# Up-projection of a gated-linear-attention encoder: the two features of a group half a group apart

## The chip, the cores and the metric

The kernel runs on one core of one Trainium2 chip. The metric is the device time of one execution in microseconds (us); the median of three runs is taken. All matmuls are float32 split by hand into a high and a low part (hi, lo), three matmuls for one product.

## What is computed

One encoder layer on a sequence of 2048 tokens of 1024 numbers: a gated linear attention, then a feed-forward net with a causal convolution, each with a norm and a residual, and a last norm. The change lies in the feed-forward net:

```python
def causal_dwconv(u, w, b):
    K = w.shape[0]
    L = u.shape[1]
    up = jnp.pad(u, ((0, 0), (K - 1, 0), (0, 0)))
    out = up[:, K - 1:K - 1 + L] * w[K - 1] + b
    for k in range(K - 1):
        out = out + up[:, k:k + L] * w[k]
    return out

def conv_ffn(h, w_up, conv_w, conv_b, w_down):
    u = causal_dwconv(h @ w_up, conv_w, conv_b)
    g, val = jnp.split(u, 2, axis=-1)
    return (jax.nn.silu(g) * val) @ w_down
...
    x = x + conv_ffn(h, ffn_w_up[i], ffn_conv_w[i], ffn_conv_b[i], ffn_w_down[i]).astype(x.dtype)
return rmsnorm(x, final_norm_w)
```

w_up has 1024 x 5632 entries, w_down 2816 x 1024, the convolution three taps.

## The kernel before

**Stages.** The attention's projections run as four passes (R, A, B, Y) over eight pairs of 128-token tiles; then comes the up-projection (`phase_u`), from 894 us on, and from about 1790 us the down-projection with the last norm. Every large matrix product is done by Winograd's form of Strassen's scheme: a product of 2 x 2 blocks by seven block products p1 to p7 in place of eight, with sums and differences of blocks as operands. A block product is 12 matmuls of 128 x 128 by 128 x 512 (`mm3p`, lines 177 to 179: four steps of the contraction, three matmuls each).

**The up-projection.** The sequence is done in two halves (s = 0, 1) of 1024 tokens. In a half, 22 features are worked, a feature being 128 gate columns with the 128 value columns that belong to them; two features make a group (11 groups). The tokens' operands, one of two hi/lo tiles for each of the seven products, stay on chip for a half (`hop`, filled by `load_op` from the scratch `hd`, 2 MB a product). The weights' operands are made in place: `load` brings four raw 128 x 512 blocks a feature (`ur`), and `prep` forms the sum or difference on POOL, casts the high part on ACT (line 186) and takes the low part on DVE (line 187, `split`). `prep` runs five products ahead.

**Order before.** In a group the order is p1, p5, p6, p7, p4, p2, p3, each for the even feature and then for the odd one. Two PSUM banks collect a feature: bank a takes p1, p6, p7 and p4, one on top of the other, bank c takes p5 and then p3; p2 has a bank of its own. Between the steps the running sums are read out: ACT copies bank a after p1 (c1), p6 (c2) and p7 (u3) and, after p4, into the value's tile; DVE adds make the even or odd 128-token blocks of the gate's u and of the value's u. A matmul that adds to a bank must wait until the read of the step before is done.

**Convolution.** When a feature's value (after p4) or gate (after p3) is complete, `conv` follows at once: one ACT activation (last tap and bias, line 1235), two DVE taps (line 1237), and for the gate a silu on ACT (line 1239). After the gate's, `gated` multiplies (line 1244), stores two blocks of the result to the scratch `ad` and, for an odd feature, forms four sums on POOL and stores them for the down-projection.

**The second half's operands.** While the first half runs, `prep_h2` makes the operands of the second half from the tokens' rows: for each of four pairs of tiles nine steps (a load, seven operands, a last store), with a difference and a low part on DVE and a cast on ACT. `spread` deals them out by a clock that the program keeps for itself while it is written out (`adv`, `later_do`): the first step 14.0 us behind the opening of the buffers, then one each 11.0 us (`U0`, `U1`), wherever that falls in the group. Their results lie in the ring of six tiles "as", which the POOL sums and u3 use too, and are stored to `hd` by DMAs that ACT issues.

**Queues.** Each engine carries out its instructions in the order in which the program issues them, DMA issues among them: an issue that must wait holds up what the program put behind it on that engine. SP issues the raw loads, the operand loads and the stores of `ad`; ACT issued the stores of `hd`.

**The ends.** The operands of the first half are loaded during the last pass Y, in that pass's order of products (p1, p5, p6, p7, p4, p2, p3). Near the end of the second half `d_early` starts the down-projection: loads of w_down into operand tiles that are free, and four prepared steps.

## Time and profile before

| | us |
| --- | --- |
| median of three runs | 2225.44 |
| lowest and highest run | 2217.04, 2226.30 |
| profiled execution, its own time | 2224.22 |
| its span, first to last instruction | 2222.5 |
| mean granted TensorE clock | 0.986 |

A row of the chain or of the timeline gives start, duration (both us), engine, line, operation, the tile written and those read, shape and count; the bracket is the engine's idle time before it and what ended it. A row of groups gives count, busy time, mean duration in ns and the idle time before. A row of the waits gives who waited for whom, the total in us, how often, and the longest. A row by stretch gives start and end, length, then for each engine the busy time and the number of instructions, at the end the granted TensorE clock, the DMA engines' busy share and GB/s. PE is TensorE (PEld its weight loads), DVE VectorE, ACT ScalarE, POOL GpSimd, SP the sync engine; a q behind the name means its sequencer, which issues DMAs.

### The profile page before, as it was taken

How to read it: one execution, taken by the hardware profiler on the slowest of the kernel's cores; microseconds unless marked ns; L12 is line 12 of the kernel's file. 1: busy time of each engine (PE TensorE's matmuls, PEld its weight loads, DVE VectorE, ACT ScalarE, POOL GpSimd, SP SyncE). 2: the span in 40 equal slices, each digit the busy share in tenths (PEclk: the TensorE clock that was granted, in tenths of full speed). 3: DMA queues.
4: the chain of work that ended last, by engine and by line, in shares of the span. 5: the costliest groups of instructions: out<-in, count | busy, mean ns of one | idle time of the engine just before them, and what ended most of it. 6: DMA issues, size and time to landing. Idle time of an engine off the chain costs nothing.

```text
span 2222.5 us, 29090 instructions
## 1 busy us (share of the span) xinstructions
PE 2122.4 (95%) x9952; PEld 1743.6 (78%) x9952; DVE 1636.5 (74%) x2167; ACT 1107.9 (50%) x2024; POOL 733.1 (33%) x602
## 2 busy tenths in 40 slices
PE   6999999989998999898999999999999999999998
PEld 5888787877887787677887777788888887888886
DVE  8655787789778765488899786897877777457564
ACT  5554755565556676444555453454554443333342
POOL 1000011111111000355566664656555435036100
PEclk9999999999999999999999999999999999999999
DMA  6645684478557889935435348433332468354453
GB/s 210 218 165 182 203 264 157 131 223 299 164 161 235 283 321 352 315 117 174 155 120 193 105 139 288 142 112 102 103 111 85 159 243 289 128 180 152 142 176 113
DMA packets 305125, 411.78 MB, mean 185 GB/s; under 512 B 23742, under 2 KB 160110, under 8 KB 304976
## 3 DMA queue, kind: packets, MB, share of 16 engines
q1 hardware_dynamic: 267440, 346.99, 47.2%
q10 hardware_dynamic: 37536, 62.93, 8.4%
q8 instruction: 78, 1.28, 0.2%
q14 instruction: 71, 0.58, 0.1%
HBM read 266.70 MB, written 143.13 MB: 184 GB/s over the span
## 4 chain that ended last, share of the span: by engine, by line
PE 62%; DVE 14%; DMA 9%; issue 7%; ACT 3%; POOL 3%; SPq 1%; ACTq 0%; DVEq 0%; POOLq 0%
PE ua L177 5%; PE pd_p L178 5%; PE pd_p L179 5%; PE pd_p L177 5%; PE ua L179 5%; PE ua L178 5%; DVE t L1237 4%; PE uc L177 2%; PE uc L179 2%; PE uc L178 2%; PE mp_R L177 2%; PE mp_R L179 2%; PE mp_R L178 2%; PE mp_Y L177 2%; PE mp_Y L179 2%
## 5 line engine op out<-in xcount | busy, mean ns | idle before, releaser
L177 PE MATMUL ua<-h_p,uw_p 128*128 128x512 f32 x704 | 280.2, 398 | 23.6 <-ACT c L1219 23.6
L178 PE MATMUL ua<-h_p,uw_p 128*128 128x512 f32 x704 | 278.6, 396 | 0.0
L179 PE MATMUL ua<-h_p,uw_p 128*128 128x512 f32 x704 | 278.4, 395 | 0.0
L1237 DVE SCALAR_TENSOR_TENSOR t<-u,cw,t 128x1024 f32<-128x1024 f32 x176 | 263.3, 1500 | 8.9 <-ACT t L1235 7.9
L178 PE MATMUL pd_p<-dw_p,da 128*128 128x512 f32 x616 | 240.5, 390 | 3.1 <-DVE da L187 3.1
L179 PE MATMUL pd_p<-dw_p,da 128*128 128x512 f32 x616 | 240.1, 390 | 0.0
L177 PE MATMUL pd_p<-dw_p,da 128*128 128x512 f32 x616 | 240.1, 390 | 0.0
L187 DVE TENSOR_TENSOR uw_p<-ur,uw_p 128x512 fp32r<-128x512 f32 x176 | 168.3, 972 | 58.5 <-ACT uw_p L186 53.3
L187 DVE TENSOR_TENSOR da<-da_p,da 128x512 fp32r<-128x512 f32 x154 | 133.6, 920 | 105.4 <-ACT da L186 105.3
L186 ACT CAST da<-da_p 128x512 fp32r<-128x512 f32 x154 | 85.2, 619 | 208.9 <-PE pd_p L179 153.3
L177 PEld LDWEIGHTS ua<-h_p,uw_p 128*128 128x128 f32 x704 | 134.1, 191 | 57.2 <-ACT c L1219 27.6
L186 ACT CAST uw_p<-us 128x512 fp32r<-128x512 f32 x132 | 82.1, 622 | 165.8 <-POOL us L1199 108.3
L187 DVE TENSOR_TENSOR uw_p<-us,uw_p 128x512 fp32r<-128x512 f32 x132 | 120.4, 921 | 57.6 <-ACT uw_p L186 57.2
L179 PEld LDWEIGHTS ua<-h_p,uw_p 128*128 128x128 f32 x704 | 134.0, 190 | 30.1
L178 PEld LDWEIGHTS ua<-h_p,uw_p 128*128 128x128 f32 x704 | 134.3, 191 | 29.5
L177 PE MATMUL uc<-h_p,uw_p 128*128 128x512 f32 x352 | 138.3, 393 | 1.0 <-DVE t L1237 1.0
L179 PE MATMUL uc<-h_p,uw_p 128*128 128x512 f32 x352 | 138.0, 392 | 0.0
L178 PE MATMUL uc<-h_p,uw_p 128*128 128x512 f32 x352 | 138.0, 392 | 0.0
L178 PEld LDWEIGHTS pd_p<-dw_p,da 128*128 128x128 f32 x616 | 116.0, 188 | 28.0 <-DVE da L187 3.9
L1235 ACT ACTIVATE t<-u,cw 128x1024 f32<-128x1024 f32 x88 | 109.8, 1247 | 51.2 <-DVE u L1328 43.3
L179 PEld LDWEIGHTS pd_p<-dw_p,da 128*128 128x128 f32 x616 | 116.0, 188 | 24.2
L177 PEld LDWEIGHTS pd_p<-dw_p,da 128*128 128x128 f32 x616 | 115.9, 188 | 24.0
(269 smaller groups left out, 5476.2 us busy)
## 6 DMA issues: line engine op xcount, KB each, us to landing
ur<-in_ffn_w_up_dram SPq DMA_DIRECT2D x168, 256.0 KB, 3.7
da_p<-ad_p SPq DMA_DIRECT2D x154, 256.0 KB, 4.1
h_p<-hd_p SPq DMA_DIRECT2D x56, 512.0 KB, 8.1
ad_p<-as_p SPq DMA_DIRECT2D x88, 256.0 KB, 2.7
ad_p<-t SPq DMA_DIRECT2D x66, 256.0 KB, 3.5
x<-in_x_dram SPq DMA_DIRECT2D x32, 512.0 KB, 4.3
ch<-in_ffn_w_down_dram SPq DMA_DIRECT2D x61, 256.0 KB, 4.4
hr_A_p<-h1d_p SPq DMA_DIRECT2D x56, 256.0 KB, 2.7
```

What stands on the lines that cost most here:

```text
L177: nc.tensor.matmul(ps_ap, ah, bl, start=(first and i == 0), stop=False, **kw)
L178: nc.tensor.matmul(ps_ap, al, bh, start=False, stop=False, **kw)
L179: nc.tensor.matmul(ps_ap, ah, bh, start=False, stop=(last and i == len(pairs) - 1), **kw)
L186: nc.scalar.copy(hi, src)
L187: nc.vector.tensor_sub(lo, src, f32(hi))
L1235: nc.scalar.activation(t, u[:, 2:2 + TS], AF.Identity, scale=cw[:, 2, c:c + 1], bias=cw[:, 3, c:c + 1])
L1237: nc.vector.scalar_tensor_tensor(t, u[:, k:k + TS], cw[:, k, c:c + 1], t, op0=ALU.mult, op1=ALU.add)
```

## The change

- **Order.** Each product gets a place. A feature's seven products lie two places apart, in the order p1, p5, p6, p2, p3, p7, p4. An even feature begins at 14 places a group, the odd one 7 places later (3 in the very first group); so the two take turns, and in the steady state the order is, with F the odd feature of the group before, E the even and O the odd one: E p1, F p3, E p5, F p7, E p6, F p4, E p2, O p1, E p3, O p5, E p7, O p6, E p4, O p2. The second half begins 7 places later, when the first is done.
- **Read-outs.** p5's sum is now copied by ACT (c5). p7's add on DVE reads bank a itself, together with c5, and the copy u3 is gone. c2 lies in the ring "out".
- **Later convolution.** `conv` and `gated` are not issued behind p3 or p4 but behind the product after it (`todo`, `late`).
- **Raw blocks** are loaded by feature, not by group, as soon as p7 and p4 of the feature two before are prepared.
- **Second half's operands** go by place: one step each at places 0, 4 and 11 of a group, from the second group on. Their stores are issued by SP.
- **Buffers.** Two u tiles in place of three; the convolution's tiles are split by gate (four) and value (one); the last two tiles' blocks of rows use the tiles hb2.
- **Down-projection.** `d_early`, the operand slots and the first banks follow the new order; of the second half's operand loads, those of p7 and p4 are issued by ACT.

```diff
-    Y0, Y1, U0, U1 = 3.0, 2.8, 14.0, 11.0
+    Y0, Y1 = 3.0, 2.8
+    H2AT = (0, 4, 11)
+    OFF0, OFF = 3, 7
...
-            t = hb2_tile(f"hb2_{tt}_{k}") if tt < TT else cp_tile(f"hb3_{tt}_{k}")
+            t = hb2_tile(f"hb2_{tt}_{k}") if tt < TT or tt + 2 >= NTT else cp_tile(f"hb3_{tt}_{k}")
...
-                        nc.scalar.dma_start(hd[s, o, j][:, i, :], f32(hl[i]))
+                        nc.sync.dma_start(hd[s, o, j][:, i, :], f32(hl[i]))
...
-        jobs = [(s, g, o, f) for s in range(NS) for g in range(NQ) for o in OPS for f in (2 * g, 2 * g + 1)]
...
+        order = []
+        for s in range(NS):
+            for f in range(2 * NQ):
+                off = 0 if f % 2 == 0 else OFF0 if s == 0 and f == 1 else OFF
+                p0 = s * (14 * NQ + OFF) + 14 * (f // 2) + off
+                order += [(p0 + 2 * i, s, f // 2, o, f) for i, o in enumerate(("p1", "p5", "p6", "p2", "p3", "p7", "p4"))]
+        order.sort()
+        jobs = [v[1:] for v in order]
+        h2at = [14 * g + v for g in range(1, NQ) for v in H2AT]
...
+            if o in ("p7", "p4"):
+                load(s, f + 2, ("p7", "p4").index(o))
...
-            u = pools["us"].tile([P, TS + 2], F32, tag="u", name=f"u_{s}_{c}", bufs=3)
+            u = pools["us"].tile([P, TS + 2], F32, tag="u", name=f"u_{s}_{c}", bufs=2)
...
-            if k % GJ in (2, 7) and k // GJ + 1 < NS * NQ:
-                load(k // GJ + 1, int(k % GJ == 7))
             if k > 3:
                 ls, lg, lo_, lf = jobs[k - 3]
-                if ls + 1 < NS and lg == NQ - 1 and lf % 2 == 1:
-                    need(*(f"h2p{jj}" for jj in range(PAIRS, 2 * PAIRS)))
-                    load_op(ls + 1, lo_)
+                if ls + 1 < NS and lf == 2 * NQ - 1:
+                    assert not h2u
+                    load_op(ls + 1, lo_, nc.scalar if lo_ in ("p7", "p4") else nc.sync)
...
+            if h2u and order[k][0] >= h2at[0]:
+                h2at.pop(0)
+                h2u.pop(0)()
+                while h2u and len(h2u) % 9 in (0, 1):
+                    h2u.pop(0)()
...
+            late, todo = todo, []
...
             elif o == "p5":
                 c = bank["c", f] = aux_ps(f"uc_{s}_{f}")
                 mm3p(c, pairs)
+                made["p5", f] = copied(cp_tile(f"c5_{s}_{f}"), c)
...
+            elif o == "p3":
+                c = bank.pop(("c", f))
+                mm3p(c, pairs, first=False, more=True)
+                nc.vector.tensor_add(made.pop(("od", f)), tiles1(c), tiles1(made.pop(("u2", f))))
+                todo.append(lambda s=s, f=f: conv(s, 0, f))
             elif o == "p7":
                 a = bank["a", f]
                 mm3p(a, pairs, first=False, more=True)
-                u3 = pools["us"].tile([P, 512], F32, tag="as", name=f"c3_{s}_{f}", bufs=AB)
-                nc.scalar.copy(u3, a)
-                ev, od = new_u(s, 1, f)
-                made["ev", f] = ev
-                nc.vector.tensor_add(od, tiles1(bank["c", f]), tiles1(u3))
-            elif o == "p4":
+                made["ev", f], od = new_u(s, 1, f)
+                nc.vector.tensor_add(od, tiles1(a), tiles1(made.pop(("p5", f))))
+            else:
                 a = bank.pop(("a", f))
                 mm3p(a, pairs, first=False, more=True)
                 nc.scalar.copy(made.pop(("ev", f)), tiles1(a))
-                conv(s, 1, f)
...
+                todo += [lambda s=s, f=f: conv(s, 1, f), lambda s=s, f=f: gated(s, f)]
+            for fn in late:
+                fn()
+        for fn in todo:
+            fn()
```

In the down-projection:

```diff
-            wgrp[o] = slots(("p7", "p4", "p3")[q // 4], f"dw_{o}_{q}")
+            wgrp[o] = slots(("p2", "p3", "p7")[q // 4], f"dw_{o}_{q}")
...
-            wgrp["a"] = slots(("p6", "p2")[k // 4 % 2], f"da_{k}")
+            wgrp["a"] = slots(("p6", "p4")[k // 4 % 2], f"da_{k}")
...
-        if o == "p6":
-            load_chain()
+        if o in ("p5", "p6"):
+            load_chain(("p5", "p6").index(o))
+        elif o == "p2":
+            d_load(4)
+        elif o == "p3":
+            d_prep(2)
         elif o == "p7":
-            d_load(4)
-        elif o == "p4":
-            d_prep(2)
-        elif o == "p3":
             d_prep(4)
...
-        banks = [(mm_ps if n % 2 == 0 else aux_ps)(f"pd_{o}_{s}_{m}") for m in range(PAIRS)]
+        banks = [(aux_ps if n % 2 == 0 else mm_ps)(f"pd_{o}_{s}_{m}") for m in range(PAIRS)]
```

## The prediction

> **What bounds the kernel now.** I read the page's first part, then who waited for whom on PE, then the busy time by stretch.

> ```profile
> PE 2122.4 (95%) x9952; PEld 1743.6 (78%) x9952; DVE 1636.5 (74%) x2167; ACT 1107.9 (50%) x2024; POOL 733.1 (33%) x602
> ...
> PE ua L177 <- ACT c L1219: 23.6, 9, 5.0
> PE ub L177 <- issue: 4.6, 1, 4.6
> ...
> core 0: us, PE busy (x) PEld busy (x) DVE busy (x) ACT busy (x) POOL busy (x), PEclk, DMA share, GB/s
> 930.00:1355.00 425.00, 406.21 (x1731) 328.87 (x1731) 357.86 (x352) 207.59 (x314) 256.39 (x204) 0.98 0.48 152
> 1355.00:1400.00 45.00, 39.35 (x160) 31.35 (x159) 29.79 (x30) 18.41 (x27) 20.36 (x18) 0.92 0.87 291
> 1400.00:1780.00 380.00, 380.00 (x1657) 310.59 (x1656) 303.67 (x298) 187.54 (x281) 217.24 (x158) 1.00 0.36 111
> ...
> 1400.00:1440.00 40.00, 40.00 (x176) 32.66 (x175) 35.43 (x29) 19.89 (x30) 29.56 (x20) 1.00 0.35 104
> ```

> PE bounds, and the changed stage (the up-projection, 308 products of 12 matmuls, 894 to about 1790 us) is almost full. Undisturbed, 176 matmuls take 40.00 us, so a product takes 12 x 40.00/176 = 2.73 us. The most the change can win is read from the stretches. 1400:1780 is full and shows 1657 records, 0.2293 us each (a few records are missing everywhere, so I compare like with like). At that pitch the 1731 records of 930:1355 need 397.0 us and took 425; the 160 of 1355:1400 need 36.7 and took 45. So **28.0 + 8.3 = 36.3 us** are lost behind 930, and nothing from 1400 on. The rows of the waits say where: ACT's copy c is late, once the operands at the boundary between the two halves of the sequence.

> ```profile
> 961.27 3.98 ACTq L823 DMA_DIRECT2D hd_p<-h2p_p  x2
> ...
> 965.29 0.59 ACT L1219 COPY c<-ua 128x512 f32<-128x512 f32 x1 [4.05 <-DVE h2p_p L187]
> ...
> 1251.60:1258.40 6.80, 5.78 (x14) 4.52 (x15) 2.04 (x3) 2.85 (x6) 0.53 (x1) 0.50 0.93 280
> ...
> 1009.89 0.50 PE L177 MATMUL ua<-h_p,uw_p 128*128 128x512 f32 x1 [2.50 <-ACT c L1219]
> ...
> 1009.80:1016.00 6.20, 6.11 (x27) 5.03 (x28) 3.97 (x6) 3.02 (x7) 0.69 (x1) 1.00 0.91 283
> ...
> 1869.91 0.79 PE L178 MATMUL pd_p<-dw_p,da 128*128 128x512 f32 x1 [2.51 <-DVE da L187]
> ...
> 1869.40:1872.80 3.40, 2.89 (x7) 2.31 (x8) 3.40 (x3) 0.00 (x0) 3.40 (x3) 0.50 0.14 39
> ```

> The 965 stall: ACT's queue sits 3.98 us on two hd_p stores that wait for DVE's low part, and the copy queued behind them starts 4.05 us late. The window rows show the second price of a stall: after it the granted clock is 0.50 for 3.4 or 6.8 us, so 1.7 us or more are lost again. A stall of 2.50 us (1009.89) kept the clock at 1.00, one of 2.51 us (1869.91) did not.

> **What the change takes away.** The hd_p stores go to SP, the copies of p7 leave the ring of six "as" buffers, and c1 has four products before p6 needs its bank. The hop loads of the second half are issued three products behind the last use and, as the halves no longer overlap, eight (p1) to four (p2) products ahead of need, 10.9 us at the least against 8.1 to landing (row below): I count all 36.3 us as won. The 56 stores (two for each of 28 steps) now wait for DVE in SP's queue; behind them stand the raw loads. These have four products (10.9 us) to the operand's preparation and five more to its product, where even a hop load lands in 8.1, so I price them at nothing; if the cover went, each group would pay a few us. The eight hop loads put on ACT's queue come behind the half's last products, where ACT has its whole second half (188 of 380 us busy) free: nothing. Counts stay: four ACT copies and three DVE adds a feature, 14 prepared operands a group. Two u tiles for three are enough, since a new one is taken three products behind the last tap on the one two before.

> **What it adds: a wait of PE on DVE, once a feature.** Before, p7 left its bank by an ACT copy (u3) and p4 came two products later. Now DVE's add reads p7's bank itself, and p4, which accumulates into that bank, still comes two products later. What is queued ahead of that add? With the other feature half a group off, the order round it is: p3 of F, p5 of G, p7 of F, p6 of G, p4 of F. The convolution of F's first half (conv, i = 0) is put behind p5 of G. So ACT's program is: copy of p5 (waits for PE), activation t, silu, cast of the next operand; DVE's: two taps L1237, low part of that operand, then the add for p7. The silu waits for the taps, the cast stands behind the silu, the low part needs the cast, and the add stands behind the low part. p4 waits for all of it. The pieces:

> ```profile
> 1420.67 0.40 PE L179 MATMUL ua<-h_p,uw_p 128*128 128x512 f32 x1
> 1420.90 0.39 PE L177 MATMUL ua<-h_p,uw_p 128*128 128x512 f32 x1
> ...
> 1421.10 0.59 ACT L1219 COPY c<-ua 128x512 f32<-128x512 f32 x1 [0.65 <-PE ua L179]
> 1421.58 0.62 ACT L186 CAST uw_p<-us 128x512 fp32r<-128x512 f32 x1
> ...
> 1391.25 1.24 ACT L1235 ACTIVATE t<-u,cw 128x1024 f32<-128x1024 f32 x1
> ...
> 1392.52 1.28 DVE L1237 SCALAR_TENSOR_TENSOR t<-u,cw,t 128x1024 f32<-128x1024 f32 x1 [1.07 <-ACT t L1235]
> 1393.72 0.68 DVE L187 TENSOR_TENSOR uw_p<-ur,uw_p 128x512 fp32r<-128x512 f32 x1
> ...
> 1242.17 1.27 DVE L1237 SCALAR_TENSOR_TENSOR t<-u,cw,t 128x1024 f32<-128x1024 f32 x1
> ...
> 1243.47 1.06 ACT L1239 ACTIVATE t<-t 128x1024 f32<-128x1024 f32 x1 [1.07 <-DVE t L1237]
> 1244.44 0.60 ACT L186 CAST uw_p<-ur 128x512 fp32r<-128x512 f32 x1
> ...
> 1390.11 0.62 ACT L186 CAST uw_p<-ur 128x512 fp32r<-128x512 f32 x1 [10.20 <-DMA ur<-in_ffn_w_up_dram]
> ...
> 1390.76 0.69 DVE L187 TENSOR_TENSOR uw_p<-ur,uw_p 128x512 fp32r<-128x512 f32 x1 [9.97 <-ACT uw_p L186]
> ...
> 1396.72 0.68 DVE L1310 TENSOR_TENSOR u<-ub,c 128x512 f32<-128x512 f32 x1
> ...
> 1251.99 0.58 ACT L1219 COPY c<-ua 128x512 f32<-128x512 f32 x1
> ...
> 1252.62 0.79 PE L177 MATMUL ua<-h_p,uw_p 128*128 128x512 f32 x1 [4.05 <-ACT c L1219]
> ```

> Counted from the first matmul after p5 (1420.90): the copy starts at 0.20, the next ACT instruction 0.48 later, the activation takes 1.25 and the tap starts 0.03 after it; first tap 1.20 to the second, second 1.28; silu 0.03 later and 0.97 to the cast, cast 0.62, low part 0.03 later, 0.61 to the add (the step from the row at 1393.72 to the next DVE instruction is as short), add 0.68, and PE 0.05 after it. Sum **7.43 us**. PE has two products, 5.46 us, to fill it: it stalls 1.97 us, and no later product can pass p4. That is with POOL out of the way. With it:

> ```profile
> L1237 DVE SCALAR_TENSOR_TENSOR t<-u,cw,t 128x1024 f32<-128x1024 f32 x176 | 263.3, 1500 | 8.9 <-ACT t L1235 7.9
> ...
> 1431.62 4.15 DVE L1237 SCALAR_TENSOR_TENSOR t<-u,cw,t 128x1024 f32<-128x1024 f32 x2 [0.45 <-ACT t L1235]
> ...
> 1432.52 2.17 POOL L1202 TENSOR_TENSOR ur<-ur 128x512 f32<-128x512 f32 x1
> ...
> L187 DVE TENSOR_TENSOR uw_p<-us,uw_p 128x512 fp32r<-128x512 f32 x132 | 120.4, 921 | 57.6 <-ACT uw_p L186 57.2
> ```

> Two taps met by POOL took 4.15 us in place of 2.48. On the mean a tap takes 1.50 (0.22 more than alone) and a low part 0.92 (0.24 more): the chain becomes 7.43 + 0.44 + 0.24 = 8.11 and the stall 2.65. The wait is bounded by 1.97 below and by about 3.9 above (both taps met, 1.67 more, and the mean low part). POOL is busy 57% of 1400:1780, and its preparation of the next operands falls partly into the chain, so I take the mean row, 2.65. It holds for 20 features of the first half and 21 of the second (not for the very first and the two last, below): 41 x 2.65 = **+109 us** (41 x 1.97 = 81 as the lower end).

> The half clock comes on top: between none and all of 41 x 1.7 = 70 us. Of the two stalls of 2.5 us quoted one was followed by it; the chain's own are of that size, and the one in the changed stage was not. I take a quarter, 10 x 1.7 = **+17 us**. [...]

> **Edges.** At the start, p2 becomes the sixth product and p3 the eighth, but the hop operands are still loaded in the order p1 p5 p6 p7 p4 p2 p3.

> ```profile
> 902.03 18.38 SPq L886 DMA_DIRECT2D h_p<-hd_p  x12
> ...
> 914.51 0.52 SPq L886 DMA_DIRECT2D h_p<-hd_p  x1
> ...
> h_p<-hd_p SPq DMA_DIRECT2D x56, 512.0 KB, 8.1
> ...
> 912.27 0.39 PE L177 MATMUL ua<-h_p,uw_p 128*128 128x512 f32 x1
> ...
> 927.11 0.39 PE L177 MATMUL ua<-h_p,uw_p 128*128 128x512 f32 x1
> ...
> L1244 DVE TENSOR_TENSOR t<-t,t 128x1024 f32<-128x1024 f32 x20 | 25.5, 1274 | 0.0
> ```

> The last twelve issues are p4's, p2's and p3's; 914.51 is the eighth, p2's last, and lands 8.1 us later at 922.6. The sixth product could start at 912.27, so it waits 10 us (before, the seventh waited here, for a copy). With three products and some 2.5 us of half clock the ninth starts at 933.3 in place of 927.11: **+6 us**. The first feature's chain has no copy ahead and is 0.9 over: +0.9. The last feature of each half runs alone, p7 directly before p4. DVE must first do two taps (3.0), the gated product (1.27), one add and two low parts: some 2.2 us over the 5.46 of p3 and p7: +2.2. In the second half eight low parts for the down-projection take the place of the two; the six more (0.61 to 0.92 each, 4.6 at the middle) make it 6.8, and a half clock between 1.7 and 2.9 comes on top: +9. The later stages keep their work; the down-projection's banks and slots are only renamed to what is free, and the last two tiles' blocks in other buffers only free the copies' ring.

> **Sum**, against the profiled execution (2224.2 us, 1.2 below the median of the runs shown, so left as it is): 2224.2 - 36.3 + 6 + 0.9 + 109 + 17 + 2.2 + 9 = **2332 us**.

> **Rivals.**
> 1. Faster: the activation t does not wait behind the copy of p5. One place decides, ACT's order between the two. If t went as soon as the add of p3 is done (0.9 us into G's p5), taps, silu, cast and low part would end 4.2 us after that product's end and the add at 4.9, under the 5.46 at which p4 starts. No stall: 2224.2 - 36.3 + 6 + 2.2 + 9 = 2205. For it: DVE has 20% of its time free from 1400 on. Against: ACT's rows above run in the program's order, copies that wait for PE included. 10%.
> 2. No change: the silu doesn't stand ahead of the cast, so 1.75 us leave the chain (0.03 + 0.97 + 0.62 + 0.03, and the tap's overlap): 5.7, a stall of 0.24, 10 us in all: 2216. Against: the silu at 1243.47 and the cast 0.97 behind it are in that order. 8%.
> 3. Slower still: each stall is followed by a half clock: 70 in place of 17, 2385. It decides from stalls of about 2.5 us up. 12%.
> 4. The forecast, 2332, 70%. Its own range is 2287 (POOL out of the way, no half clock) to 2375 (a half clock after six in seven of the stalls).

> **How the numbers follow.** About 0.5% (11 us) is what a measurement of this kernel can tell from no change. Rival 1 is faster (0.10), rival 2 within (0.08), the forecast and rival 3 slower (0.82). The range takes the forecast's whole own range and most of rival 3, 2400 at the top; at the bottom it reaches to 2230 for gains and waits that I mis-sized.

> **What would show it.** In the waits, a new row of PE on ua from DVE's add of p7 (u), some 41 times, 2 to 3 us each, all at the first matmul of p4; the copy c row nearly gone; ub from the load h_p at the start, some 10 us. In the timeline before such a stall: copy, t, two L1237, L1239, cast, low part, add. In 1400:1780 PE would be busy some 90% instead of all. The prediction is wrong if that row is missing or under 1 us each, or if the ninth product starts at 927.

## The result and the profile after

| | before | after |
| --- | --- | --- |
| median (runs) | 2224.31 us (4) | 2278.82 us (4; 2275.62 to 2281.45) |
| ratio, 95% interval | | 1.0254 (1.0236 to 1.0273) |
| profiled execution: time, span | 2224.22, 2222.5 | 2279.15, 2277.2 |
| mean granted TensorE clock | 0.986 | 0.980 |

The change makes the kernel 54.5 us slower; the forecast was 108 slower. First the waits of PE from 870 to 1870 us (who waited for whom, total, times, longest) in the kernel after:

```profile
PE ua L179 <- DVE u L1340: 57.8, 22, 3.9
...
PE ub L179 <- DMA h_p<-hd_p: 4.7, 2, 3.2
...
PE uc L179 <- DMA h_p<-hd_p: 2.2, 1, 2.2
```

The row that was forecast is there: the first matmul of p4 waits for DVE's add of p7, and the copy row of before is gone. But it comes 22 times, not 41. Its mean, 57.8 / 22 = 2.63 us, is the forecast's 2.65. Next the stretches of the kernel after:

```profile
930.00:1380.00 450.00, 417.06 (x1763) 338.15 (x1761) 374.40 (x358) 212.36 (x318) 262.59 (x209) 0.97 0.45 144
1380.00:1440.00 60.00, 50.89 (x199) 40.50 (x199) 34.75 (x36) 22.35 (x33) 23.53 (x20) 0.91 0.71 246
1440.00:1815.00 375.00, 353.75 (x1514) 288.22 (x1515) 303.39 (x274) 172.75 (x255) 204.69 (x146) 0.98 0.31 95
```

At the 0.2293 us a record that the prediction worked out, these 1763, 199 and 1514 records need 404.3, 45.6 and 347.2 us. So 45.7, 14.4 and 27.8 us are lost, 87.9 in all, where the kernel before lost 36.3. Of the 87.9, PE stood idle for 63.3 (32.94 + 9.11 + 21.25, each stretch less PE's busy time). The other 24.6 us is busy time above 0.2293 a record, the half clock (the granted clock of the three stretches is 0.97, 0.91 and 0.98). The same two parts before were 24.4 and 11.9. The new loss is therefore about 39 us of idling and 13 of clock.

The rest of the bill is at the two ends. PE's timeline, after:

```profile
919.26 0.50 PE L179 MATMUL ua<-h_p,uw_p 128*128 128x512 f32 x1 [3.79 <-ACT uw_p L188]
...
927.53 0.77 PE L179 MATMUL ub<-h_p,uw_p 128*128 128x512 f32 x1 [1.47 <-DMA h_p<-hd_p]
...
934.19 0.39 PE L180 MATMUL ub<-h_p,uw_p 128*128 128x512 f32 x1
...
1849.56 0.39 PE L181 MATMUL ua<-h_p,uw_p 128*128 128x512 f32 x1
```

The record that stood at 927.11 before (the 97th of the stage) stands at 934.19, 7.1 us later. The stage's last matmul is at 1849.56; before it was at 1789.79. From the 97th record to the last it is 915.4 in place of 862.7 us: +52.7. Behind it the spans leave 427.6 and 432.7 us: -5.1, because the down-projection's first matmuls now run between the stage's last. 7.1 + 52.7 - 5.1 = 54.7, the difference of the two spans.

**Why every second feature.** PE's matmuls of the stage can be counted off in products of twelve, in the order that the change gives. By that count 18 of the 22 stalls stand at the p4 of an even feature, one in each group from the second to the tenth of both halves: 3.3 to 3.6 us in the first half, 2.1 in the second. The other four stand at the ends of the halves: at the first two features of the first half (1.25 and 0.77 us), at its last feature (3.89) and at the second feature of the second half (2.47). Here are one even and one odd feature in the second half, first on DVE (kernel after; start, duration, operation, and in brackets the idle time before it):

```profile
1579.13 2.32 DVE L1257 TENSOR_TENSOR t<-t,t 128x1024 f32<-128x1024 f32 x1
...
1581.97 0.68 DVE L1334 TENSOR_TENSOR u<-uc,c 128x512 f32<-128x512 f32 x1
...
1583.96 4.26 DVE L1250 SCALAR_TENSOR_TENSOR t<-u,cw,t 128x1024 f32<-128x1024 f32 x2 [0.21 <-ACT t L1248]
1588.15 1.76 DVE L189 TENSOR_TENSOR uw_p<-us,uw_p 128x512 fp32r<-128x512 f32 x1
1589.83 0.68 DVE L1340 TENSOR_TENSOR u<-ua,c 128x512 f32<-128x512 f32 x1
...
1605.49 2.61 DVE L1250 SCALAR_TENSOR_TENSOR t<-u,cw,t 128x1024 f32<-128x1024 f32 x2 [0.71 <-ACT t L1248]
1608.01 0.68 DVE L189 TENSOR_TENSOR uw_p<-us,uw_p 128x512 fp32r<-128x512 f32 x1
1608.61 0.68 DVE L1340 TENSOR_TENSOR u<-ua,c 128x512 f32<-128x512 f32 x1
```

POOL beside the even one:

```profile
1581.53 1.68 POOL L1271 TENSOR_TENSOR as_p<-t,t 128x512 f32<-128x512 f32 x1
1583.29 1.63 POOL L1275 TENSOR_TENSOR as_p<-as_p,t 128x512 f32<-128x512 f32 x1
1585.00 2.15 POOL L1273 TENSOR_TENSOR as_p<-t,as_p 128x512 f32<-128x512 f32 x1
1587.11 2.25 POOL L1275 TENSOR_TENSOR as_p<-t 128x512 f32<-128x512 f32 x1
```

ACT beside it:

```profile
1582.69 1.25 ACT L1248 ACTIVATE t<-u,cw 128x1024 f32<-128x1024 f32 x1 [1.71 <-DVE u L1334]
1583.83 0.57 ACT L1232 COPY c<-uc 128x512 f32<-128x512 f32 x1
1584.30 0.62 ACT L188 CAST uw_p<-us 128x512 fp32r<-128x512 f32 x1
1588.26 1.06 ACT L1252 ACTIVATE t<-t 128x1024 f32<-128x1024 f32 x1 [3.34 <-DVE t L1250]
```

And PE, at the p4 of the even feature and at that of the odd one:

```profile
1590.57 0.50 PE L179 MATMUL ua<-h_p,uw_p 128*128 128x512 f32 x1 [2.11 <-DVE u L1340]
...
1609.82 0.39 PE L179 MATMUL ua<-h_p,uw_p 128*128 128x512 f32 x1
```

The gated product of the odd feature (L1257) has just been made, so POOL forms its four sums, 1581.53 to 1589.36, beside the taps of the even feature. The taps take 4.26 us where the odd feature's take 2.61, and the low part 1.76 where that one's takes 0.68. The add ends at 1590.51 and PE has stood for 2.11 us. At the odd feature no sums run, the add ends at 1609.29 and PE's next p4 starts at 1609.82 without a wait.

The sums alone are not enough, however. In the last group of each half they run beside the even feature's taps too, and there is no stall. DVE there, in the second half:

```profile
1823.52 1.22 DVE L1257 TENSOR_TENSOR t<-t,t 128x1024 f32<-128x1024 f32 x1
...
1827.81 3.80 DVE L1250 SCALAR_TENSOR_TENSOR t<-u,cw,t 128x1024 f32<-128x1024 f32 x2 [0.66 <-ACT t L1248]
...
1833.24 0.68 DVE L1340 TENSOR_TENSOR u<-ua,c 128x512 f32<-128x512 f32 x1
```

And PE:

```profile
1833.98 0.50 PE L179 MATMUL ua<-h_p,uw_p 128*128 128x512 f32 x1
```

The two taps take 3.80 us and the low part 1.78, nearly as long as above. But the gated product takes 1.22 us in place of 2.32. At the other features POOL prepares two operands at that place (at the even one above from 1576.97 to 1580.37), beside a low part (1.79 us) and the gated product; here POOL stood idle for 5.05 us before 1823.13. So the add of p3 starts right behind PE's p3, not 1.7 us later, and the add of p7 ends at 1833.92, in time. At the odd features it is the other way round: POOL prepares ahead (the gated product takes 2.31 us), but no sums follow. Neither meeting makes the stall by itself; both in one chain do. This is read from three places of one run; no experiment took the preparation alone away.

ACT's rows show the second difference from the prediction. The activation t stands ahead of the copy of p5, and the cast stands ahead of the silu. So ACT does not work in the order of the program's text; the order was set when the program was built, and there too it is t, copy, cast, silu.

### The profile page after: what moved, and what is told of

The parts are those of the page before. It is cut to its first block, busy times and chain, and to the rows that moved or that the text cites. A ratio compares the mean times of both kernels' runs of the same rounds, so it can differ in the third digit from the quotient of the medians.

```text
span 2277.2 us, 28999 instructions
## 1 busy us (share of the span) xinstructions
PE 2134.1 (94%) x9952; PEld 1751.5 (77%) x9952; DVE 1669.3 (73%) x2167; ACT 1111.9 (49%) x2024; POOL 741.1 (33%) x602
## 3 DMA queue, kind: packets, MB, share of 16 engines
q8 instruction: 78, 1.28, 0.2%
## 5 line engine op out<-in xcount | busy, mean ns | idle before, releaser
L179 PE MATMUL ua<-h_p,uw_p 128*128 128x512 f32 x704 | 286.3, 407 | 62.4 <-DVE u L1340 57.8
L180 PE MATMUL ua<-h_p,uw_p 128*128 128x512 f32 x704 | 282.8, 402 | 0.2 <-DVE uw_p L189 0.2
L181 PE MATMUL ua<-h_p,uw_p 128*128 128x512 f32 x704 | 281.8, 401 | 0.0
L189 DVE TENSOR_TENSOR uw_p<-ur,uw_p 128x512 fp32r<-128x512 f32 x176 | 183.4, 1044 | 96.3 <-ACT uw_p L188 96.3
L179 PE MATMUL pd_p<-dw_p,da 128*128 128x512 f32 x616 | 239.6, 389 | 0.0
L179 PEld LDWEIGHTS ua<-h_p,uw_p 128*128 128x128 f32 x704 | 136.3, 194 | 103.5 <-DVE u L1340 68.8
L181 PEld LDWEIGHTS ua<-h_p,uw_p 128*128 128x128 f32 x704 | 137.0, 195 | 30.2
L180 PEld LDWEIGHTS ua<-h_p,uw_p 128*128 128x128 f32 x704 | 137.1, 195 | 28.5 <-DVE uw_p L189 0.5
L1208 POOL TENSOR_TENSOR us<-ur,ur 128x512 f32<-128x512 f32 x44 | 68.8, 1565 | 223.7 <-DMA ur<-in_ffn_w_up_dram 204.8
L179 PE MATMUL uc<-h_p,uw_p 128*128 128x512 f32 x352 | 138.5, 394 | 2.2 <-DMA h_p<-hd_p 2.2
L180 PEld LDWEIGHTS pd_p<-dw_p,da 128*128 128x128 f32 x616 | 115.6, 188 | 26.2 <-DVE da L189 2.2
L189 DVE TENSOR_TENSOR uw_p<-us,uw_p 128x512 fp32r<-128x512 f32 x132 | 112.3, 851 | 31.5 <-ACT uw_p L188 29.8
L663 POOL TENSOR_TENSOR r<-r,gnw 128x512 f32<-128x512 f32 x32 | 48.6, 1520 | 264.3 <-ACT r L662 222.6
L179 PEld LDWEIGHTS pd_p<-dw_p,da 128*128 128x128 f32 x616 | 115.6, 188 | 24.2
## 6 DMA issues: line engine op xcount, KB each, us to landing
h_p<-hd_p SPq DMA_DIRECT2D x48, 512.0 KB, 8.3
x<-in_x_dram SPq DMA_DIRECT2D x32, 512.0 KB, 4.9
```

Source lines behind the costliest of these rows:

```text
L179: nc.tensor.matmul(ps_ap, ah, bl, start=(first and i == 0), stop=False, **kw)
L180: nc.tensor.matmul(ps_ap, al, bh, start=False, stop=False, **kw)
L181: nc.tensor.matmul(ps_ap, ah, bh, start=False, stop=(last and i == len(pairs) - 1), **kw)
L189: nc.vector.tensor_sub(lo, src, f32(hi))
L663: nc.gpsimd.tensor_mul(r, r, sp["gnw"])
L1208: add(src, a21, a22)
```

## The experiments

**Theory A**: POOL's four sums meet the taps and the low part ahead of the add, and that makes the add late. **Its first rival**: the cost is the direct read of the bank, in place of an ACT copy. Each edit below is against the changed kernel unless it says otherwise. The kernel before ran beside them, with medians from 2221.22 to 2223.40 us.

**1. Put the copy back.** ACT copies p7's bank, and the add reads the copy; PE then waits for the copy alone.

```diff
+                u3 = copied(pools["us"].tile([P, 512], F32, tag="as", name=f"c3_{s}_{f}", bufs=AB), a)
...
-                nc.vector.tensor_add(od, tiles1(a), tiles1(made.pop(("p5", f))))
+                nc.vector.tensor_add(od, tiles1(u3), tiles1(made.pop(("p5", f))))
```

> The changed kernel with p7's bank read by an ACT copy again (u3), the DVE add then reads that copy and c5. Theory A (the stall of PE at p4 of each even feature comes from the gate's two taps standing ahead of what reads the bank, and from POOL's four sums slowing these taps): ACT's copy stands behind the silu, and the silu behind the taps, so the wait stays, 22 times, only named after ACT's copy and some 0.7 us shorter each (low part 0.61 and add 0.68 replaced by the copy 0.58): the 57.8 us of PE on the add become about 42, time 2255 to 2270. Rival R1 (the price is the direct read of the bank by DVE): the stalls go, time about 2278.8 - 57.8 - 15 of half clock = 2206.

Measured: 2247.14 us, ratio 1.0102 (1.0087 to 1.0117). PE now waits for the copy:

```profile
PE ua L179 <- ACT c L1232: 42.1, 23, 6.9
```

The waits are the 42 us of theory A; the time is 8 us under its range and far above the first rival's 2206. The stalls keep their number and get shorter, so the direct read accounts for part of the loss (some 32 us of time) and is not the cause by itself: something also makes the copy late.

**2. No sums on POOL.** The four sums are left out; single blocks are stored in their place.

```diff
-            for o, fn, x, y in (("p5", "add", a21, a22), ("p6", "sub", None, a11), ("p3", "rsub", None, a12), ("p7", "sub", a11, a21)):
...
+            for o, x in (("p5", a21), ("p6", a11), ("p3", a12), ("p7", a22)):
+                nc.sync.dma_start(tiles1(ad[s, o, q]), x)
```

> The changed kernel without POOL's four sums of the gated product of each group: other blocks are stored in their place, so this leaves out part of the operands of the down-projection. Theory A: the even features' taps take 1.28 each as the odd features' do, the add of p7 ends some 0.4 us before p4 could start; PE's 57.8 us on that add fall under 10, time 2200 to 2215. R1: without POOL's work the 22 stalls stay at 2 us or more, over 40 us in all, time over 2255.

Measured: 2219.05 us in a single run, 4 us above theory A's range. The row on DVE falls from 57.8 us and 22 times to this:

```profile
PE ua L179 <- DVE u L1330: 14.3, 8, 2.5
```

That is over the 10 us that theory A allowed, but what is left lies before 1050 us and at the ends of the halves; from 1410 to 1785 us there is no such wait. So the sums are needed for the stalls that recur. What this run doesn't say is by which way, since DVE's room, POOL's room and SP's stores change together.

**3. The sums later.** They are held until the add of p7 of the next even feature, by a copy of two columns from its result, which the sum then overwrites.

```diff
+            made["sums"] = (s, q, made.pop(("a", 0)), made.pop(("a", 1)))
+
+        def sums_of(u=None):
+            s, q, (a11, a21), (a12, a22) = made.pop("sums")
...
+                if u is not None and o in ("p5", "p7"):
+                    nc.gpsimd.tensor_copy(t[:, 0:2], u[:, 2 + P:4 + P])
...
+                if f % 2 == 0 and "sums" in made:
+                    sums_of(made["u", 1, f])
```

> The changed kernel with the four sums of a group held back until the next even feature's add of p7 is done (two columns of its output are copied first into the tiles of the first and last sum, which are then overwritten), so that they no longer meet that feature's taps. Nothing is left out. Theory A: as without the sums, 57.8 us of waits fall under 12, time 2203 to 2220, under the kernel before. R1: over 2255. Rival R3 (the sums only move to the next feature's taps): the stalls pass to the odd features, 2 us each, time about 2270.

Measured: 2271.69 us, ratio 1.0219 (1.0198 to 1.0239). PE's row on DVE keeps 57.5 us, 23 times: a miss for theory A. But the stalls have changed places. Counted by products, all from 955 us on stand at odd features: 1.5 to 5.1 us in the first half, 8.4 at its end, 5.7 at the first odd feature of the second half and 0.6 to 1.3 after that. At the even features the add is now in time, as theory A has it. Place and time (2270 us) are those of rival R3, though not for its reason: the sums end at 1565.41 us and don't meet the odd feature's taps. DVE at that odd feature:

```profile
1572.25 3.75 DVE L1250 SCALAR_TENSOR_TENSOR t<-u,cw,t 128x1024 f32<-128x1024 f32 x2 [0.72 <-ACT t L1248]
```

POOL's rows there show what came instead:

```profile
1571.32 1.37 POOL L1208 TENSOR_TENSOR us<-ur,ur 128x512 f32<-128x512 f32 x1 [3.67 <-DMA ur<-in_ffn_w_up_dram]
1572.76 2.15 POOL L1214 TENSOR_TENSOR ur<-ur 128x512 f32<-128x512 f32 x1
```

SP's queue in the same place:

```profile
1559.46 6.29 SPq L1283 DMA_DIRECT2D ad_p<-as_p  x4
1565.84 2.11 SPq L1198 DMA_DIRECT2D ur<-in_ffn_w_up_dram  x4
```

The stores of the held sums stand on SP for 6.29 us, the raw loads go behind them, and POOL waits 3.67 us for its block. So its preparation begins 5.2 us ahead of the add of p7, where it began 10.1 us ahead at the odd feature of the changed kernel, and falls beside the taps, which take 3.75 us in place of 2.61. The block of work was moved onto another path, not taken away.

**4. The taps later.** The gate's convolution is tied behind the add of p7 (again by two columns), so that the sums can no longer lengthen the taps ahead of it.

```diff
+            if i == 0 and (s or f > 1):
+                nc.vector.tensor_copy(t[:, 0:2], made["u", 1, f][:, 2 + P:4 + P])
...
+                if s or f > 1:
+                    conv(s, 0, f)
```

> The changed kernel with the gate's convolution tied behind the add of p7: DVE copies two columns of that add's output into the convolution's tile, which ACT then overwrites, so the activation, the taps and the silu can only run behind the add (from the third feature on). Theory A: the add has nothing but low parts ahead of it and ends well before p4; PE's 57.8 us on the add fall under 10 and the half clock behind the stalls goes too: 2205 to 2222, at or under the kernel before. Rival R4 (DVE is too full at that place, whatever the order): the taps then delay the adds of the other feature, PE stalls there, 2240 or more.

Measured: 2279.75 us, ratio 1.0263 (1.0244 to 1.0283); PE waits 62.0 us for DVE, 23 times: a miss. The stalls that recur stay at the even features, 1.4 to 5.1 us each, and do not pass to the other feature as R4 has it. DVE at an even feature:

```profile
1621.81 1.21 DVE L189 TENSOR_TENSOR uw_p<-us,uw_p 128x512 fp32r<-128x512 f32 x1 [4.30 <-ACT uw_p L188]
1622.94 0.68 DVE L1343 TENSOR_TENSOR u<-ua,c 128x512 f32<-128x512 f32 x1
```

POOL at the same time:

```profile
1618.61 1.29 POOL L1277 TENSOR_TENSOR as_p<-t 128x512 f32<-128x512 f32 x1
1619.86 1.27 POOL L1208 TENSOR_TENSOR us<-ur,ur 128x512 f32<-128x512 f32 x1
```

ACT:

```profile
1621.16 0.62 ACT L188 CAST uw_p<-us 128x512 fp32r<-128x512 f32 x1 [5.63 <-POOL us L1208]
```

The taps are out of the way, and DVE has nothing to do for 4.30 us. Yet the add is no earlier than before: PE stalls 3.33 us here. In DVE's queue a low part stands ahead of it; that needs ACT's cast, the cast needs POOL's operand sum L1208, and this stands behind the four sums. Theory A falls in the form "the taps are lengthened". What these runs leave is **theory B**: POOL's block of four sums holds back whatever DVE has ahead of the add, through the taps or through the next operand.

**5. The sums on DVE**, nothing else moved. This separates the engine from the place.

```diff
-                    nc.gpsimd.tensor_add(tv, x, y)
+                    nc.vector.tensor_add(tv, x, y)
...
-                    nc.gpsimd.tensor_sub(tv, y, last)
+                    nc.vector.tensor_sub(tv, y, last)
...
-                    nc.gpsimd.tensor_sub(tv, last if x is None else x, y)
+                    nc.vector.tensor_sub(tv, last if x is None else x, y)
```

> The four sums of a group are made on DVE in place of POOL, nothing else is moved. Theory B (POOL's block of four sums at the even feature is what makes the add of p7 late there, by whichever way it takes): the block is gone from POOL, so the taps near it go back to 1.28 us and POOL's operand sums come at once; DVE has four adds of about 0.68 us more a group, which may stand ahead of the add of p7 and cost up to 2.7 us there in place of the 2.0 to 2.5 that the contention took. Waits of PE on DVE's u between 15 and 60 us; a time between 2215 and 2280. Rival C (any 2.7 us of work behind the gated product at that place makes the add late, whoever does it): the 22 waits stay, 45 to 60 us, 2265 to 2285. Near the lower ends it is POOL alone; near the upper ends it is the place.

Measured: 2233.60 us, ratio 1.0058 (1.0038 to 1.0078), 45 us less than the changed kernel. PE's waits:

```profile
PE ua L179 <- DVE u L1340: 28.7, 27, 2.9
```

DVE at an even feature:

```profile
1587.44 0.68 DVE L1271 TENSOR_TENSOR as_p<-t,t 128x512 f32<-128x512 f32 x1
...
1590.45 0.68 DVE L1275 TENSOR_TENSOR as_p<-t 128x512 f32<-128x512 f32 x1
1591.05 1.27 DVE L1250 SCALAR_TENSOR_TENSOR t<-u,cw,t 128x1024 f32<-128x1024 f32 x1
...
1594.04 0.67 DVE L1340 TENSOR_TENSOR u<-ua,c 128x512 f32<-128x512 f32 x1
```

All four sums (the first and the last are shown) stand ahead of the add and cost DVE 4 x 0.68 = 2.7 us; still PE's stall there is 0.85 us in place of 2.1, since a tap is back at 1.27. Rival C, that the place decides whoever works there, is refuted in its size: 28.7 us of waits and 2233.60 us lie well under its 45 to 60 and 2265 to 2285. The 0.85 us is what the place still costs.

**6. The sums on DVE and held**, with the edits of 3 and 5 together.

> The four sums on DVE and held until the add of p7 of the next even feature (each sum's tile gets a 2-column copy from that add's result first), so that neither POOL's block nor DVE's adds stand ahead of the add. Theory B and rival C both expect the waits of PE on DVE's u to fall to under 20 us, as without the sums (14.3), and a time of 2215 to 2235: the copies add some 0.06 us each, and DVE has the room. If raw blocks come late because SP's stores of the held sums stand ahead of their loads (as with the sums held on POOL), the first half shows waits on the operand uw_p instead and the time stays above 2245. If the waits on u stay at about 57 us with neither block ahead of the add, both fall.

Measured: 2232.85 us, ratio 1.0050 (1.0032 to 1.0069); PE waits 24.1 us, 17 times, somewhat over the 20 that both expected. From 1440 us on PE has no wait of over 0.5 us for the add, so it is in time there with neither block ahead of it. The first half keeps stalls of 0.7 to 3.5 us, at odd features as in 3, and one of 5.5 at the boundary; why each of them comes was not followed up. A two-column copy on DVE took 0.15 us where experiment 4 has one (at 1624.84), not 0.06.

**7. The sums on DVE, and the copy back**: the edits of 1 and 5 together.

> The changed kernel with the four sums on DVE and p7's bank read by an ACT copy again (u3), with the add behind it. The stalls that the sums on DVE left in the second half (0.85 us at each even feature) should go, since the copy alone took off about 0.8 us each before: waits of PE on bank a from DVE and ACT together under 20 us (28.7 with the sums on DVE alone, 42.1 with the copy alone). The time is 2215 to 2225: the start and the boundary stay as they are (about +7 and the loads h_p). If the copy u3 is itself held on the ring that the sums use, waits on ACT c of 20 us or more and 2230 to 2240.

Measured: 2222.78 us, ratio 0.9996 (0.9982 to 1.0009): level with the kernel before. PE waits 21.8 us for the copies, 19 times, slightly over the bound of 20, and no longer than 0.5 us at a time behind 1420 us.

**8. The stores of hd back on ACT** (in the changed kernel), and **9. on SP in the kernel before**.

```diff
-                        nc.sync.dma_start(hd[s, o, j][:, i, :], f32(hl[i]))
+                        nc.scalar.dma_start(hd[s, o, j][:, i, :], f32(hl[i]))
```

> The changed kernel with one part undone: ACT issues the stores of the second half's operands again. If a store that waits for DVE in ACT's queue is what made the copies late in the kernel before, the first half gets worse, by some 5 to 20 us (with the kernel before, the same move was worth 4.4 us): 2283 to 2299, with waits of PE on an ACT copy of one of the banks. If the fixed places alone keep the stores clear of the copies: within 4 us of 2278.8.

> The kernel before with one part of the change alone: SP issues the stores of the second half's operands. Theory A on the gain (ACT's copies were late because ACT's queue stood on stores that wait for DVE): of the 23.6 us of PE on the copy c the stalls at 965, 1009, 1052, 1252 and 1296 shrink to what the ring of six tiles leaves, 10 to 18 us less with the half clock: 2206 to 2216. Rival: the waits pass to SP and the raw blocks come late: 2224 or more.

Measured: 8 gives 2280.51 us, ratio 1.0264 (1.0249 to 1.0280), with 57.4 us of waits on DVE: nothing changes. 9 gives 2218.98 us, ratio 0.9979 (0.9969 to 0.9988), and leaves 21.1 of the 23.6 us of waits on copies. That is between the two expectations. At the 965 stall that the prediction quoted, 4.99 us became 0.84, but a wait of 3.23 us came at the next feature. So the stores in ACT's queue were a small part of the late copies.

**10. The kernel before with the sums on DVE**, by the edit of 5.

> The kernel before with the four sums on DVE in place of POOL, nothing of the change in it. It says what that edit is worth without the changed order, where no p4 waits two products behind p7 for an add. If POOL's sums matter only through the wait that the change added, the time stays within 0.5% (2212 to 2234) and the copy waits stay near 21 to 24 us. If late copies there come from sums that meet DVE too, those waits fall to about 10 and the time to 2195 to 2212. With DVE 2.7 us a group more loaded at the group's end it could also go up to 2240.

Measured: 2212.65 us, ratio 0.9955 (0.9936 to 0.9975), the fastest of all. It gains 9 us, where the same edit gained 45 in the changed kernel; PE's waits on the copies fall only from 23.6 to 20.7 us, so the gain isn't in that row alone. Without the change's wait, POOL's sums cost little. Against this kernel, 7 is still 10 us slower. In the two profiled executions, 13.6 us apart, 4.5 us of that lie ahead of the stage's 97th matmul, 6.3 from there to the stage's end and 2.8 behind it; no run took these apart.

## Why the prediction was right in its sign and too large

**The new wait: right, its count wrong.** "p4 waits for all of it" is the row of 57.8 us, at the place and with the mean that were given. The term that was mis-sized is 41 x 2.65 = 109: it measured 22 x 2.63 = 57.8, with the boundary's stall in it. The mean agrees by two errors that cancel. Only 18 of the 41 features that were to stall did, 3.4 us each on the mean in the first half and 2.1 in the second; the other four stalls stand at the ends. So the time fell below the forecast's own range (2287 to 2375), and that it lies above the kernel before is in good part luck: with the order that was built, the prediction's own rivals 1 and 2 forecast 2205 and 2216.
- The step "ACT's program is: copy of p5, activation t, silu, cast" failed. t ran 1.14 us ahead of the copy, and the cast ran 3.96 ahead of the silu (rows at 1582.69 to 1588.26). Both conditions, that of rival 1 and that of rival 2, held; at the odd features the chain then ended 0.53 us early and cost nothing, as rival 1 says.
- The meeting with POOL was priced by mean rows (0.44 and 0.24 us). It doesn't fall evenly: at the even feature the two taps took 4.26 us, 1.65 more than at the odd one, and the low part 1.76, 1.08 more. Against the odd feature these 2.73 us put the add too late; the even feature of the last group, where POOL prepares nothing ahead, shows that they do so only on top of the earlier meeting. Not every operation grew: the taps and the low part did, POOL's last two sums took 2.15 and 2.25 us (in the rows of experiment 4, where DVE is idle, a sum took 1.29 and an operand 1.27), and the add at 1581.97, which reads a PSUM bank, stayed at 0.68 beside POOL's first sum. Why these grow and that one doesn't can't be read from these rows.

In the first half a stall that recurs is 1.3 us longer than in the second (3.4 for 2.1). The operands of the second half are in the chain there, which the prediction had not counted; the rows show it, no run took it apart. DVE, kernel after:

```profile
1104.99 1.78 DVE L189 TENSOR_TENSOR h2p_p<-h2r,h2p_p 128x512 fp32r<-128x512 f32 x1
1106.70 4.54 DVE L1250 SCALAR_TENSOR_TENSOR t<-u,cw,t 128x1024 f32<-128x1024 f32 x2
...
1112.37 0.68 DVE L1340 TENSOR_TENSOR u<-ua,c 128x512 f32<-128x512 f32 x1
```

**The 36.3 us that were counted as won: only in part.** The waits on copies are gone, but the boundary lost 14.4 us where it had lost 8.3. The step "eight (p1) to four (p2) products ahead of need" failed there. SP's queue at the boundary, after:

```profile
1359.81 6.59 SPq L1277 DMA_DIRECT2D ad_p<-as_p  x4
...
1382.29 19.57 SPq L888 DMA_DIRECT2D h_p<-hd_p  x11
```

SP stood for 6.59 us on the stores of the sums, and the last eleven loads went out from 1382.29 to 1401.86, one each 1.78 us, with the DMA engines busy all that time (share 1.00, 359 GB/s). The prediction took 8.1 us to landing for a load and had no such queue in it. PE waited 3.2 and 2.2 us for them; the add's stall of 3.9 us stands there too. Experiment 7 comes out level with the kernel before and not 36 us under it, but it can't show the gain: with p7's copy back, PE waits 21.8 us for copies again. No run here has the gain without a new wait.

**Half clock: near.** It cost 24.6 us behind 930; the forecast had 17 there, and some 2 in the tails. Rival 3, a half clock after every stall, didn't come: of the second half's nine stalls that recur three were followed by one (at 1466.78, 1507.74 and 1712.54).

**The start: +7.1 for +6, by luck.** Of the 7.1 us, 5.7 are a later beginning of the stage (899.41 for 893.73), which the prediction did not have and no run explains. p2, the forecast's sixth product, waited 1.47 us for its operand, not 10, because the built order put it seventh, and a wait of 3.79 us for an operand's cast came ahead of it. **The tails** (+2.2, +9): the first half's last feature stalled 3.9 us; the second half's last one not at all, and the overlap with the down-projection gave 5.1 back. **The raw loads behind SP's stores** cost PE no wait for an operand behind the stage's start, as forecast; experiment 3 shows the cover going.

## What to carry to other kernels

Where a chain on DVE decides, look for the places at which POOL works through a block of elementwise work, and price the meetings there along the whole chain, from rows of two operations that met (here two taps of 4.26 us, and 2.61 where no sums ran). A mean over the stage hid here that 18 of the 22 stalls stood at even features, and that two meetings in one chain cost 2.11 us where either alone cost none. Take each engine's order from a built program or a trace, not from the text, before a chain is added up along it. Before a block is moved to another time, try it on another engine: of the two, only the second took most of the cost away here (2233.60 us; moved, 2271.69; neither, 2278.82).

## What the runs showed of the hardware

In the kernel after, the half clock (0.50) behind three of the second half's stalls comes in stretches of 3.41 us that begin at 1466.78, 1507.74 and 1712.54 us; the distances, 40.96 and 204.80, are 12 and 60 times 3.413. So the stage is cut here into windows of that length, counted on from 1466.78. Here are two stalls, of 2.08 and 2.10 us, cut into such windows (stretches, kernel after; the first number behind the length is PE's busy time, the third from the end the granted clock):

```profile
1463.37:1466.78 3.41, 1.36 (x6) 1.14 (x7) 3.31 (x3) 2.41 (x4) 2.72 (x3) 1.00 0.25 94
1466.78:1470.19 3.41, 3.41 (x10) 2.64 (x9) 0.69 (x1) 0.34 (x2) 1.28 (x1) 0.50 0.54 159
...
1545.29:1548.70 3.41, 2.51 (x12) 1.74 (x10) 3.38 (x3) 1.10 (x2) 3.41 (x3) 1.00 0.36 134
1548.70:1552.11 3.41, 2.21 (x10) 1.82 (x11) 3.14 (x4) 1.57 (x3) 1.91 (x3) 1.00 0.21 77
1552.11:1555.53 3.42, 3.42 (x17) 2.83 (x16) 0.92 (x2) 2.25 (x3) 1.24 (x1) 1.00 0.51 153
```
